# Grouped RMS norm of a two-layer hybrid decoder: one product with a matrix of 1/512 instead of two small steps, and the power of all 256 columns on GpSimd

## The chip, the cores and the metric

The kernel runs on one core of one Trainium2 chip. The time is that of one execution on the device in microseconds (us), from the first to the last instruction and what the runtime adds around it; less is better. The engines are named as in the profile: PE multiplies matrices (PEld loads its weights), DVE is VectorE, ACT is ScalarE, POOL is GpSimd, SP issues the loads.

## What is computed

Two layers, each on 256 tokens of width 1024. One input projection feeds an attention group (eight heads) and a state space group (SSD, sixteen heads); both results are gated, joined and multiplied by `w_out`. The change is in the norm that the SSD half passes before `w_out`. It works in two groups of 512 channels:

```python
y = y * jax.nn.silu(z.astype(jnp.float32))
y = rms_norm(y.reshape(b, s, SSD_GROUPS, D_SSD // SSD_GROUPS),
             ssd_norm_w.reshape(SSD_GROUPS, D_SSD // SSD_GROUPS))
...
mixed = jnp.concatenate([attn, y], axis=-1)
return x + mixed @ w_out
```

`rms_norm` multiplies by `lax.rsqrt(mean(x * x) + EPS)` and by a weight for each channel. For every token and group there is so one mean of 512 squares and one power of -0.5.

## The kernel before

Activations lie with channels on the 128 partitions and the 256 tokens along the free dimension. The SSD result is the tile `x2` (eight blocks of 128 channels by 256 tokens; the profile calls it `x`, as it calls the residual tile `x_sb`): group 0 is blocks 0 to 3, group 1 is blocks 4 to 7.

**Products in three parts.** A large product is made of three products each: activation and weight are split in a rounded part and a rest (`hT`/`lT`, `ah`/`al`, `sh`/`sl` for activations, `wh`/`wl` for weights), and high by high, low by high and high by low are added up in PSUM (lines 222 to 224, 240 to 242). ACT rounds each weight block from `raw` to `wh` (line 99), DVE subtracts to get `wl` (line 100). `Weights.pump` keeps at most eight blocks (`NB`) prepared that PE has not yet finished with; a block is two slices of 128 rows by up to 512 columns.

**Order of a layer's end.** The gates of attention are computed (`g`), then the gates of the SSD half (`z`, lines 653 to 659, four passes). After passes 1 and 3 the generator `group_norm` starts for group 0 and group 1. Then come the products with `w_out`: first all that need only the attention half (`oa0`, `oa1`: 96 products from `ah`, `al`), then `drain()` ends what generators are open, then 24 products `ob` (blocks 0 and 1 of `sh`, `sl`) and 72 products `oc` (blocks 2 to 7). In `oc` the first six products of a result take blocks 2 and 3, the rest blocks 4 to 7, which are group 1. The results lie in four tiles `o`; in the last layer one of them is cut in two of 256 columns, and the second half is called `o11b`.

**The norm itself.** `group_norm` (line 506) has three stages, divided by `yield 3` and `yield 2`, which put the next stage so many ticks later (a tick follows each weight block of PE). Stage one: ACT squares the four blocks (`ysq`), DVE adds the four (`sr`, 128 partitions by 256 tokens). Stage two: PE multiplies `sr` with a column of ones, which sums the 128 partitions and puts the tokens on the partitions (`np`, two products of one column each); DVE divides by 512 and adds epsilon (`nv`); POOL raises two columns to -0.5 (`rn`, helper `rpow`, line 181); DVE makes a diagonal matrix of it (`dg`). Stage three: PE multiplies `ones` by `dg`, which spreads the 256 powers to all partitions (`rg`, in PSUM); DVE multiplies each block of `x2` by the weight and by `rg` (line 533), and `split` (line 183) makes `sh` on ACT and `sl` on DVE for each two blocks.

`sr` and `dg` share one buffer (`tag="sr"`, one copy), so `sr` of group 1 waits until group 0 is done with it.

**What sets the order.** Every engine works through its own queue in order and waits by semaphores. The order in each queue is set when the program is built: a scheduler places each instruction by its own estimate of times, apart from the stretches under `manual_schedule` (the start, and PE's queue in the last `oc` products). A change in one place can therefore move instructions of other lines.

Of the kernel before, what the change touches and what calls it, by code (L numbers as in the profile page):

```python
# [9 lines left out]
F32 = mybir.dt.float32  # L10
F32R = mybir.dt.float32r
AF = mybir.ActivationFunctionType
ALU = mybir.AluOpType
AX = mybir.AxisListType

P = 128
S = 256
# [6 lines left out]
EPS = 1e-6  # L24
# [3 lines left out]
C_QN, C_KN, C_CW, C_CB, C_SW, C_DS, C_LN, C_DTB, C_AL = 0, 1, 2, 50, 62, 70, 78, 86, 102  # L28
# [91 lines left out]
def hybrid_kernel(ctx: ExitStack, tc: tile.TileContext, x, par, w, out):  # L120
    nc = tc.nc
    act, dve, pool, pe = nc.scalar, nc.vector, nc.gpsimd, nc.tensor

    const = ctx.enter_context(tc.tile_pool(name="const", bufs=1))
    keep = ctx.enter_context(tc.tile_pool(name="keep", bufs=1))
    tmp = ctx.enter_context(tc.tile_pool(name="tmp", bufs=2))
    small = ctx.enter_context(tc.tile_pool(name="small", bufs=4))
# [7 lines left out]
    def bank(name):  # L135
        return ps_s.tile([P, 512], F32, tag="ps_s", name=name)
# [4 lines left out]
    par_sb = const.tile([P, NL * NPAR], F32, name="par_sb")  # L141
# [12 lines left out]
    ones = const.tile([P, P], F32, name="ones")  # L154
# [5 lines left out]
    for i in range(WARM):  # L160
# [3 lines left out]
    io = tmp.tile([P, 512], F32, tag="th", name="io")  # L164
    pool.iota(io, pattern=[[1, 512]], base=-256, channel_multiplier=-1,
              allow_small_or_imprecise_dtypes=True)
    ident = const.tile([P, P], F32, name="ident")
    dve.tensor_scalar(ident, io[:, 256:384], 0.0, None, ALU.is_equal)
    tri = const.tile([P, 384], F32, name="tri")
# [6 lines left out]
    mhalf = const.tile([P, 8], F32, name="mhalf")  # L176
    dve.memset(mhalf, -0.5)

    def rpow(o, i):
        n = i.shape[-1]  # L180
        pool.tensor_tensor(o, i, mhalf[:, :n], ALU.pow)

    def split(h, l, src):
        act.copy(h, src)
        dve.tensor_tensor(l, src, h.bitcast(F32), ALU.subtract)
# [320 lines left out]
    def group_norm(L, g, y, sh, sl):  # L506
        pc = L * NPAR
        gs = slice(4 * g, 4 * g + 4)
        sq = tmp.tile([P, 4, S], F32, tag="sq", name="ysq", bufs=1)
        act.activation(sq, y[:, gs, :], AF.Square)  # L510
        sr = tmp.tile([P, S], F32, tag="sr", name="sr", bufs=1)
        dve.tensor_reduce(sr, sq.rearrange("p c n -> p n c"), AX.X, ALU.add)
        yield 3
        np_ = bank("np")
        for t in range(2):
            pe.matmul(np_[:, t:t + 1], sr[:, t * P:(t + 1) * P], ones[:, 0:1],
                      start=True, stop=True)
        nv = small.tile([P, 2], F32, tag="nv", name="nv")
        dve.tensor_scalar(nv, np_[:, 0:2], 1.0 / 512.0, 4.0 * EPS, ALU.mult, ALU.add)
        rn = small.tile([P, 2], F32, tag="rn", name="rn")  # L520
        rpow(rn, nv)
        dg = tmp.tile([P, S], F32, tag="sr", name="dg", bufs=1)
        for t in range(2):
            ts = slice(t * P, (t + 1) * P)
            dve.tensor_scalar(dg[:, ts], ident, rn[:, t:t + 1], None, ALU.mult)
        yield 2
        rg = bank("rg")
        for t in range(2):
            ts = slice(t * P, (t + 1) * P)
            pe.matmul(rg[:, ts], ones, dg[:, ts], start=True, stop=True)  # L530
        for c in range(4):
            ct = 4 * g + c
            dve.scalar_tensor_tensor(y[:, ct, :], y[:, ct, :],
                                     par_sb[:, pc + C_SW + ct:pc + C_SW + ct + 1], rg[:, 0:256],
                                     ALU.mult, ALU.mult)
            if c % 2:
                split(sh[:, ct - 1:ct + 1, :], sl[:, ct - 1:ct + 1, :], y[:, ct - 1:ct + 1, :])
# [3 lines left out]
    for L in range(NL):  # L541
        pc = L * NPAR
# [110 lines left out]
        for pr in range(4):  # L653
            ps = ps_p.tile([P, 512], F32, tag="ps_p", name=f"z{pr}")
            mm_pair(L, f"z{pr // 2}", pr % 2, hT, lT, ps, pr % 2 == 1)
            ys = x2[:, 2 * pr:2 * pr + 2, :]
            dve.tensor_tensor(ys, ys, silu2(ps), ALU.mult)
            if pr % 2 == 1:
                resume(group_norm(L, pr // 2, x2, sh, sl))
# [101 lines left out]
```

## Time and profile before

| | us |
|---|---|
| median of three runs (455.07 to 455.64) | 455.21 |
| the profiled execution | 456.82 |
| span of its instructions | 455.0 |
| PE busy in the span | 445.7 (98%) |
| DVE busy | 345.9 (76%) |
| ACT busy | 278.5 (61%) |
| POOL busy | 23.7 (5%) |

The profile is one execution. Its busy time counts instructions that do work, not semaphores; the end of a PE product is modelled, so products that follow each other overlap in the rows, and the distance from start to start tells the rate. A row of the timeline gives the start, the duration, the engine, the line and what is written from what; in square brackets stands the idle time before it and what ended it. DVE and POOL rows give the time of the instruction itself.

### The profile page before, as it was taken

The page shows a single profiled execution, that of the slowest core. Times are in us where ns is not written, and L with a number is a line of the kernel's source. Part 1 is how long each engine was busy: PE and PEld are TensorE (multiplying, and loading weights), DVE is VectorE, ACT ScalarE, POOL GpSimd, SP SyncE. Part 2 cuts the span into 40 slices and gives each one's busy share as a digit, 9 for nine tenths or more (in the row PEclk, how much of TensorE's full clock was granted, in tenths as well). Part 3 has the DMA queues.
Part 4 walks back from the last instruction along what each step waited for, and adds up shares of the span by engine and source line. Part 5 has one row for each costly group of instructions (what it writes and reads, how often), then busy time and mean ns, then how long its engine had stood idle before and what let it go on. Part 6 is the DMA issues. An engine that isn't in the chain of part 4 may idle for free.

```text
span 455.0 us, 7868 instructions
## 1 busy us (share of the span) xinstructions
PE 445.7 (98%) x2948; PEld 404.1 (89%) x2948; DVE 345.9 (76%) x634; ACT 278.5 (61%) x569; POOL 23.7 (5%) x29
## 2 busy tenths in 40 slices
PE   7999999999999999999999999999999999999997
PEld 6998877899998999888899878889999999998986
DVE  5597873789999998778384785676999999787621
ACT  5666775996669545445365766967667765555400
POOL 0000221200000000000000011110000000000000
PEclk9999999999999999999999999999999999999999
DMA  8868767524453445555264888651525443553301
GB/s 248 289 226 289 257 234 303 177 89 149 145 180 119 130 150 185 186 176 146 57 184 159 297 288 306 205 184 52 178 90 171 157 140 117 183 185 128 130 24 69
DMA packets 26661, 79.43 MB, mean 175 GB/s; under 512 B 2912, under 2 KB 9728, under 8 KB 26112
## 3 DMA queue, kind: packets, MB, share of 16 engines
q1 hardware_dynamic: 26192, 78.67, 52.2%
q8 instruction: 23, 0.38, 0.3%
q10 hardware_dynamic: 432, 0.27, 0.2%
q14 instruction: 14, 0.11, 0.1%
HBM read 77.85 MB, written 1.08 MB: 173 GB/s over the span
## 4 chain that ended last, share of the span: by engine, by line
PE 86%; DMA 5%; ACT 4%; DVE 3%; issue 2%; POOL 1%; ACTq 0%; SPq 0%; DVEq 0%; POOLq 0%
PE o L222 6%; PE o L223 6%; PE o L224 6%; PE xb L240 4%; PE xb L242 4%; PE xb L241 4%; PE z L241 3%; PE z L240 3%; PE z L242 3%; PE g L242 3%; PE g L240 3%; PE g L241 3%; PE yp L491 3%; PE k L222 2%; PE q L222 2%; PE k L223 2%
## 5 line engine op out<-in xcount | busy, mean ns | idle before, releaser
L100 DVE TENSOR_TENSOR wl<-raw,wh 128x1024 fp32r<-128x1024 f32 (+3 forms) x145 | 165.5, 1156 | 40.3 <-ACT wh L99 38.6
L99 ACT CAST wh<-raw 128x1024 fp32r<-128x1024 f32 (+3 forms) x145 | 143.3, 999 | 60.0 <-DMA raw<-in_w_dram 19.2
L240 PE MATMUL xb<-hT,wh 128*128 128x256 f32 x192 | 56.1, 292 | 0.0
L241 PE MATMUL xb<-lT,wh 128*128 128x256 f32 x192 | 54.4, 284 | 0.0
L242 PE MATMUL xb<-hT,wl 128*128 128x256 f32 x192 | 53.6, 279 | 0.0
L241 PEld LDWEIGHTS xb<-lT,wh 128*128 128x128 f32 x192 | 36.2, 189 | 0.3
L240 PEld LDWEIGHTS xb<-hT,wh 128*128 128x128 f32 x192 | 36.1, 188 | 0.2
L242 PEld LDWEIGHTS xb<-hT,wl 128*128 128x128 f32 x192 | 36.1, 188 | 0.1
L242 PE MATMUL g<-hT,wl 128*128 128x256 f32 x128 | 36.1, 282 | 0.0
L241 PE MATMUL z<-lT,wh 128*128 128x256 f32 x128 | 36.1, 282 | 0.0
L240 PE MATMUL g<-hT,wh 128*128 128x256 f32 x128 | 36.0, 281 | 0.0
L240 PE MATMUL z<-hT,wh 128*128 128x256 f32 x128 | 36.0, 281 | 0.0
L242 PE MATMUL z<-hT,wl 128*128 128x256 f32 x128 | 36.0, 281 | 0.0
L241 PE MATMUL g<-lT,wh 128*128 128x256 f32 x128 | 35.9, 281 | 0.0
L440 DVE SCALAR_TENSOR_TENSOR cv<-rw,par_sb,cv 128x256 f32<-128x256 f32 x72 | 31.6, 478 | 5.1 <-ACT cv L437 5.1
L222 PE MATMUL k<-wh,hT 128*128 128x512 f32 x64 | 25.5, 399 | 0.0
L223 PE MATMUL k<-wh,lT 128*128 128x512 f32 x64 | 25.3, 396 | 0.0
L224 PE MATMUL k<-wl,hT 128*128 128x512 f32 x64 | 25.3, 395 | 0.0
L222 PE MATMUL q<-wh,hT 128*128 128x512 f32 x64 | 25.3, 397 | 0.0
L223 PE MATMUL q<-wh,lT 128*128 128x512 f32 x64 | 25.0, 393 | 0.0
L224 PE MATMUL q<-wl,hT 128*128 128x512 f32 x64 | 24.7, 396 | 0.0
L222 PE MATMUL o<-wh,ah 128*128 128x512 f32 (+1 forms) x64 | 24.6, 384 | 0.0
(194 smaller groups left out, 1104.4 us busy)
## 6 DMA issues: line engine op xcount, KB each, us to landing
raw<-in_w_dram SPq DMA_DIRECT2D x120, 512.0 KB, 4.3
raw<-in_w_dram SPq DMA_DIRECT2D x15, 348.0 KB, 3.8
cb<-cd SPq DMA_DIRECT2D x4, 1024.0 KB, 7.2
raw<-in_w_dram SPq DMA_DIRECT2D x8, 344.0 KB, 3.8
x<-in_x_dram SPq DMA_DIRECT2D x2, 512.0 KB, 6.2
xT<-in_w_dram SPq DMA_DIRECT2D x3, 256.0 KB, 4.9
out_dram<-x SPq DMA_DIRECT2D x3, 256.0 KB, 2.0
raw<-in_w_dram SPq DMA_DIRECT2D x2, 174.0 KB, 3.4
```

The lines of the kernel that those rows point to most:

```text
L99: nc.scalar.copy(h[:, ks, :wd], src[:, ks, :wd])
L100: nc.vector.tensor_tensor(lo[:, ks, :wd], src[:, ks, :wd], h[:, ks, :wd].bitcast(F32), ALU.subtract)
L222: pe.matmul(ps[:, cs], lh[:, kl, tl], wh[:, kk, cs], start=first, stop=False)
L223: pe.matmul(ps[:, cs], ll[:, kl, tl], wh[:, kk, cs], start=False, stop=False)
L224: pe.matmul(ps[:, cs], lh[:, kl, tl], wl[:, kk, cs], start=False, stop=final)
L240: pe.matmul(o, wh[:, kk, cs], lh[:, k, :], start=(k == 0 and c == 0), stop=False)
L241: pe.matmul(o, wh[:, kk, cs], ll[:, k, :], start=False, stop=False)
L242: pe.matmul(o, wl[:, kk, cs], lh[:, k, :], start=False, stop=(k == KT - 1 and c == 1))
L440: dve.scalar_tensor_tensor(cv[:, c, :], rw[:, c, k:k + S], cw(k), cv[:, c, :], ALU.mult, ALU.add)
L491: pe.matmul(yp[o, c0:(i + 1) * S], xd[:, hi, xs], e_hi[:, j, :] if hi else e_lo[:, j, :], start=(hi == 0), stop=(hi == 1))
```

## The change

The sum over partitions and its spreading become one product: a 128 by 128 matrix filled with 1/512 (`ones512`) times `sr` puts the mean of each token on all partitions at once (`np`, 256 columns). DVE adds epsilon and writes the result to SBUF as `rg`, in the buffer of `sr`. POOL raises `rg` to -0.5 in place, 128 partitions by 256 columns, the exponent read from one column of `mhalf`. DVE then multiplies from this `rg`, which lies in SBUF and no longer in PSUM. The steps `nv`, `rn`, `dg` and the product `rg` are gone. `ones512` is filled once at the start.

```diff
+    ones512 = const.tile([P, P], F32, name="ones512")
+    dve.memset(ones512, 1.0 / 512.0)
...
         np_ = bank("np")
-        for t in range(2):
-            pe.matmul(np_[:, t:t + 1], sr[:, t * P:(t + 1) * P], ones[:, 0:1],
-                      start=True, stop=True)
-        nv = small.tile([P, 2], F32, tag="nv", name="nv")
-        dve.tensor_scalar(nv, np_[:, 0:2], 1.0 / 512.0, 4.0 * EPS, ALU.mult, ALU.add)
-        rn = small.tile([P, 2], F32, tag="rn", name="rn")
-        rpow(rn, nv)
-        dg = tmp.tile([P, S], F32, tag="sr", name="dg", bufs=1)
-        for t in range(2):
-            ts = slice(t * P, (t + 1) * P)
-            dve.tensor_scalar(dg[:, ts], ident, rn[:, t:t + 1], None, ALU.mult)
+        pe.matmul(np_[:, 0:S], ones512, sr, start=True, stop=True)
+        rg = tmp.tile([P, S], F32, tag="sr", name="rg", bufs=1)
+        dve.tensor_scalar(rg, np_[:, 0:S], 4.0 * EPS, None, ALU.add)
+        pool.tensor_tensor(rg, rg, mhalf[:, 0:1].to_broadcast([P, S]), ALU.pow)
         yield 2
-        rg = bank("rg")
-        for t in range(2):
-            ts = slice(t * P, (t + 1) * P)
-            pe.matmul(rg[:, ts], ones, dg[:, ts], start=True, stop=True)
         for c in range(4):
...
-                                     par_sb[:, pc + C_SW + ct:pc + C_SW + ct + 1], rg[:, 0:256],
+                                     par_sb[:, pc + C_SW + ct:pc + C_SW + ct + 1], rg,
```

The change also moves instructions of other lines, because the scheduler places them anew. Line numbers of the changed program are two higher from the helper `rpow` on and nine lower behind `group_norm`; the numbers behind the names are those of buffers.

DVE's queue in layer 1 before, from the epsilon step `nv` of group 0 on (`wl` is the weight rest, `g2z` and the `x` behind it the gate of pass 3, line 533 the norm's multiplications):

```order
L519 TENSOR_SCALAR nv<-np 128x2
L100 TENSOR_TENSOR wl_4775<-raw_4643,wh_4774 128x1024
L525 TENSOR_SCALAR dg<-ident,rn 128x128 x2
L100 TENSOR_TENSOR wl_4803<-raw_4736,wh_4802 128x1024
L503 SCALAR_TENSOR_TENSOR g2z<-thz,z_4712 128x512
L657 TENSOR_TENSOR x_1_3433<-x_1_3433,g2z 128x512
L533 SCALAR_TENSOR_TENSOR x_1_3433<-x_1_3433,par_sb,rg 128x256 x4
L512 TENSOR_REDUCE sr<-ysq 128x256
```

The same stretch of DVE's queue in the changed program:

```order
L519 TENSOR_SCALAR rg<-np 128x256
L100 TENSOR_TENSOR wl_4753<-raw_4629,wh_4752 128x1024
L100 TENSOR_TENSOR wl_4781<-raw_4714,wh_4780 128x1024
L505 SCALAR_TENSOR_TENSOR g2z<-thz,z_4693 128x512
L648 TENSOR_TENSOR x_1_3419<-x_1_3419,g2z 128x512
L100 TENSOR_TENSOR wl_4831<-raw_4732,wh_4830 128x1024
L100 TENSOR_TENSOR wl_4843<-raw_4750,wh_4842 128x1024
L100 TENSOR_TENSOR wl_4855<-raw_4778,wh_4854 128x1024
L100 TENSOR_TENSOR wl_4868<-raw_4828,wh_4867 128x1024
L524 SCALAR_TENSOR_TENSOR x_1_3419<-x_1_3419,par_sb,rg 128x256 x4
L187 TENSOR_TENSOR sl_4491<-x_1_3419,sh_4490 128x512
L514 TENSOR_REDUCE sr<-ysq 128x256
```

Four more subtractions `wl` now stand between the epsilon step and the norm's multiplications; in layer 0 it is eight more. Behind the epsilon step of group 1 stand one `wl` (layer 0, of 696 columns) and three (layer 1) ahead of the multiplications.

PE's queue in layer 0 before, around the partition sums `np` of group 1 (`ah`, `al` are the attention half):

```order
L223 MATMUL o_2421<-wh_2283,al_1718 128x512
L224 MATMUL o_2421<-wl_2284,ah_1717 128x512
L516 MATMUL np<-ones,sr 128x1 x2
L222 MATMUL o_2421<-wh_2283,ah_1717 128x512
L223 MATMUL o_2421<-wh_2283,al_1718 128x512
```

And in the changed program (`sh`, `sl` are the normed SSD half; `wh_2385` belongs to `ob`, `wh_2397` is the first block of `oc`):

```order
L225 MATMUL o_2438<-wh_2385,sl_2034 128x512
L226 MATMUL o_2438<-wl_2386,sh_2033 128x512
L224 MATMUL o_2438<-wh_2385,sh_2033 128x512
L517 MATMUL np<-sr,ones_120 128x256
L225 MATMUL o_2438<-wh_2385,sl_2034 128x512
L226 MATMUL o_2438<-wl_2386,sh_2033 128x512
L224 MATMUL o_2320<-wh_2397,sh_2033 128x512
L225 MATMUL o_2320<-wh_2397,sl_2034 128x512
```

The product `np` of group 1 stood among the products of the attention half; it now stands behind 22 products that read the normed group 0. In layer 1 it is 23 of them, and the 24 products of `o11b` from `ah` and `al` stand behind it.

## Rows read from the trace of the kernel before

**Rows 1.** The page, part 1: busy us, share and count by engine.
```profile
PE 445.7 (98%) x2948; PEld 404.1 (89%) x2948; DVE 345.9 (76%) x634; ACT 278.5 (61%) x569; POOL 23.7 (5%) x29
```

**Rows 2.** POOL's groups by shape: count | busy us, mean ns | idle before, releaser.
```profile
L181 POOL TENSOR_TENSOR rr<-se,mhalf 128x4 f32<-128x4 f32 x16 | 18.0, 1124 | 123.0 <-DVE se L337 89.7 <-DVE dt L401 33.3
L181 POOL TENSOR_TENSOR rn<-nv,mhalf 128x2 f32<-128x2 f32 x4 | 2.8, 697 | 223.7 <-DVE nv L519 223.7
L181 POOL TENSOR_TENSOR rs<-me,mhalf 128x1 f32<-128x1 f32 x4 | 2.2, 560 | 51.5 <-DVE me L256 32.1 <-DVE me L302 19.4
L165 POOL IOTA io<- 128x512 f32 x1 | 0.6, 557 | 0.4 <-POOLq L746 0.4
```

**Rows 3.** POOL's timeline: start us, us, instruction, idle before.
```profile
50.80 2.02 POOL L181 TENSOR_TENSOR rr<-se,mhalf 128x4 f32<-128x4 f32 x1 [1.56 <-DVE se L337]
...
184.54 0.69 POOL L181 TENSOR_TENSOR rn<-nv,mhalf 128x2 f32<-128x2 f32 x1 [94.52 <-DVE nv L519]
201.04 0.69 POOL L181 TENSOR_TENSOR rn<-nv,mhalf 128x2 f32<-128x2 f32 x1 [15.80 <-DVE nv L519]
...
270.51 1.01 POOL L181 TENSOR_TENSOR rr<-se,mhalf 128x4 f32<-128x4 f32 x1 [1.27 <-DVE se L337]
```

**Rows 4.** DVE's timeline at the norm of layer 0, group 0.
```profile
184.31 0.15 DVE L519 TENSOR_SCALAR nv<-np 128x2 f32<-128x2 f32 x1
184.59 1.23 DVE L100 TENSOR_TENSOR wl<-raw,wh 128x1024 fp32r<-128x1024 f32 x1
...
186.45 1.23 DVE L100 TENSOR_TENSOR wl<-raw,wh 128x1024 fp32r<-128x1024 f32 x1 [0.24 <-ACT wh L99]
...
188.31 0.69 DVE L657 TENSOR_TENSOR x<-x,g2z 128x512 f32<-128x512 f32 x1
191.52 1.66 DVE L533 SCALAR_TENSOR_TENSOR x<-x,par_sb,rg 128x256 f32<-128x256 f32 x4 [2.52 <-PE rg L530]
...
197.41 3.48 DVE L100 TENSOR_TENSOR wl<-raw,wh 128x1024 fp32r<-128x1024 f32 x3
```

**Rows 5.** DVE's timeline elsewhere: beside two powers of Rows 3, and layer 1.
```profile
50.73 1.22 DVE L100 TENSOR_TENSOR wl<-raw,wh 128x1024 fp32r<-128x1024 f32 x1
...
270.56 1.23 DVE L100 TENSOR_TENSOR wl<-raw,wh 128x1024 fp32r<-128x1024 f32 x1 [0.19 <-ACT wh L99]
...
404.97 0.15 DVE L519 TENSOR_SCALAR nv<-np 128x2 f32<-128x2 f32 x1
405.69 1.22 DVE L100 TENSOR_TENSOR wl<-raw,wh 128x1024 fp32r<-128x1024 f32 x1 [0.57 <-ACT wh L99]
```

**Rows 6.** ACT's timeline at the norm of layer 0.
```profile
189.09 1.06 ACT L510 ACTIVATE ysq<-x 128x1024 f32<-128x1024 f32 x1 [2.19 <-DVE x L657]
192.43 0.62 ACT L184 CAST sh<-x 128x512 fp32r<-128x512 f32 x1 [2.27 <-DVE x L533]
```

**Rows 7.** PE's timeline: first `ob` product and first of group 1, both layers.
```profile
208.76 0.39 PE L222 MATMUL o<-wh,sh 128*128 128x512 f32 x1
...
215.62 0.39 PE L222 MATMUL o<-wh,sh 128*128 128x512 f32 x1
...
426.71 0.28 PE L222 MATMUL o11b<-wh,ah 128*128 128x256 f32 x1
...
429.54 0.40 PE L222 MATMUL o<-wh,sh 128*128 128x512 f32 x1
...
436.47 0.39 PE L222 MATMUL o<-wh,sh 128*128 128x512 f32 x1
```

**Rows 8.** The chain in order of time: start us, us, what.
```profile
191.04 0.44 PE rg L530 x4
```

**Rows 9.** DVE's groups by shape: an operation of 256 columns that reads PSUM.
```profile
L692 DVE TENSOR_TENSOR x<-x,o 128x256 f32<-128x256 f32 x1 | 0.4, 422 | 1.4 <-PE o L224 1.4
```

**Rows 10.** The page, part 2 (granted clock, tenths), and PE's first timeline row.
```profile
PEclk9999999999999999999999999999999999999999
...
1.05 4.64 PE L161 MATMUL warm<-ones 128*128 128x128 f32 x20 [1.05 <-DVE ones L155]
```

## The prediction

> **What bounds the kernel now.** I read the page first: PE is busy for 445.7 of 455.0 us, POOL for 23.7 [rows 1]. So a change counts only where it makes PE wait or takes work from PE. Then the timelines around the two norms of each layer. In layer 0 the power `rn` of group 0 ends at 185.2 [rows 3], the norm's multiplications run from 191.52 [rows 4], and PE takes the normed blocks only at 208.76 [rows 7]: some 15 us of slack. Group 1 has its power at 201.04 [rows 3], and PE takes its first block at 215.62 [rows 7]. Nothing of the norm makes PE wait today. What the change adds must fit in that slack, or it is paid in full.
>
> **What POOL will charge.** The same operation takes 560 ns for one column, 697 for two [rows 2], and 1.01 us for four when undisturbed [rows 3] (the mean of 1124 [rows 2] holds disturbed ones as well). That is 137 ns for the second column and some 155 for each of the next two: the price of a column does not fall with length in these rows. To 256 columns: 560 + 255 x 149 (the mean step) = 38.6 us; by the last step, 1007 + 252 x 155 = 40.1 us; by the smallest, 697 + 254 x 137 = 35.5 us. I take 39.4, between the first two, as four columns are the nearest row. It stands four times, so one microsecond here is four at the end.
>
> **Group 0, layer 0.** The epsilon step starts where `nv` did, at 184.31 [rows 4]. It now writes 256 columns from PSUM: 0.42 us by the nearest such row [rows 9] in place of 0.15, so it ends at 184.73. POOL followed `nv` by 0.08 us [rows 3, 4], so the power starts at 184.81 and ends at 224.2. The first cast `sh` starts 0.91 us after the first multiplication [rows 4, 6] and takes 0.62; with 0.14 for the hand-overs from POOL to DVE and from ACT to PE (a guess, of the size of that 0.08) it is 1.67 us, so the first product with `sh` is at 225.9 and not at 208.76. PE's other work ends at about 207.7 there, as the products `rg`, 0.44 us each [rows 8], are gone. PE waits 18 us.
>
> **Group 1, layer 0.** This no longer runs beside. Its sum `sr` lies in the buffer that holds `rg` until group 0's multiplications have read it, and stands behind them on DVE; on PE its `np` stands behind 22 products that need group 0. Thirty such products took from 208.76 to 215.62 [rows 7], 0.229 each, so 22 take 5.0 and `np` runs at 230.9. A product of 256 columns is as long as the four passes of 128 of `rg`, 0.44 [rows 8]; with its pipeline I let DVE start 0.6 later. Then 0.42 + 0.08, and the power starts at 232.1 and ends at 271.5; with the 1.67 the first product of group 1 is at 273.1, which was at 215.62. PE has only eight products (1.8 us) to do meanwhile. **Layer 0 costs 57.5 us.**
>
> **Layer 1**, in its own old times: 404.97 [rows 5] + 0.42 + 0.08 + 39.4 gives 444.9, first `sh` product 446.5 (it was 429.54). Then 18 products of 512 columns and 5 of 256 (0.118 each: 24 from 426.71 to 429.54 [rows 7]), 4.7 us; then 0.6 + 0.5 + 39.4 + 1.67, which is 493.4 against 436.47 [rows 7]. **Layer 1 costs 57.0 us.** The 24 products `o11b`, now behind `np`, are done in this wait and cost nothing; on the path they would be 2.8 us.
>
> **Clock.** The page shows the full granted clock all through [rows 10]. Yet the first 20 passes of 128 columns took 4.64 us after a PE that had done nothing [rows 10], against 0.11 us each in mid-kernel [rows 8], which makes 2.2: at the start PE went at half its speed for 4 us and lost about 2. Here PE starts four times after a wait of 18 to 39 us. Lower bound 0 (the trace has no such wait), upper bound twice the row's loss, 16 in all; I take 2 each, 8 us.
>
> **What goes away** is worth almost nothing: 0.44 us of `rg` on PE and two `dg` on DVE for each group lie ahead of waits that PE now has anyway. The `memset` of `ones512` stands ahead of `mhalf` while DVE waits for POOL's first output; hidden.
>
> Sum so far, against the profiled execution's own time: 456.8 + 57.5 + 57.0 + 8 = 579.3. The median lies 1.6 below that execution, so 577.7.
>
> **What DVE does meanwhile decides the rest.** In layer 0 ten `wl` subtractions and the gate's product stand behind the epsilon step and ahead of the multiplications; all read two operands from SBUF. The row at 50.80 is a power that started 0.07 us after such a subtraction: 2.02 us instead of 1.01 [rows 3, 5]. It waited until the subtraction had read its operands. The other way round, a subtraction that started 0.05 us after a power kept its 1.23 us, though the power ran on for 0.96 [rows 3, 5], and so did the one at 184.59 [rows 4]. But these powers may have read their two or four columns at once; one of 256 columns reads for as long as it computes, unless it first copies its input. So either the two exclude each other for 39 us, or hardly at all; the trace has no power of this length. I hold exclusion the more likely, since one direction of it is seen.
>
> If they exclude each other: in layer 0 the first `wl` stands ready (it ran at 184.59 [rows 4]) and starts just before the power, which waits 1.0 us and ends at 225.2. PE meanwhile runs out of `wl` blocks near 200, but it would have waited anyway. From 225.2 DVE does one `wl`, `g2z` and `x`, 2.5 us as from 186.45 to 189.0 [rows 4], ACT squares (1.06 [rows 6]) and casts as many elements (about as long), and eight `wl` follow at 1.13 us (three took 3.48 [rows 4]), ending at 239.0. Only then come the multiplications: 14.8 us later than 224.2. Group 1 of layer 0 has one short `wl`: 0.7. In layer 1 the power wins (its `wl` waits for ACT until 405.69 [rows 5]); two `wl`, gate, square, cast, then four `wl`: 455.2 against 444.9, 10.3. Group 1 there has three `wl`: 3.4. Sum 29.2, so 608.5 by the profile, **606.9** by the median. If DVE slips in and only stops POOL for as long as it reads, the same subtractions lengthen the powers by about 24: 602.
>
> The Trainium skill, "SBUF — State Buffer", "Who interferes with whom", says that a DVE instruction with two SBUF inputs contends with a GpSimd instruction that reads SBUF, and that whoever holds the shared pair first blocks the other for the whole instruction. The row at 50.80 agrees; the row at 270.56 does not, for a power of four columns; of 256 columns no run here shows it. By the rule the time would be 606.9, without it 577.7.
>
> **Rivals.** *No exclusion*: 577.7 us, everything as above, with DVE's work hidden under the power. The row at 270.56 speaks for it [rows 5], the one at 50.80 against it [rows 3]. *A loop that is cheaper for long rows*: at a quarter of the price, 10 us, group 0 is hidden (184.8 + 10 + 1.7 is before 207.7), and group 1 waits 10.6 us in layer 0 (10 + 2.4 less 1.8 of cover) and 7.4 in layer 1 (5 of cover); with some 2 us of clock loss and 1.3 of PE work gone, 474. Against it: the steps of 137, 155, 155 ns. *Not slower*: POOL's one long instruction in the trace, 512 columns, takes 557 ns [rows 2]. If the 560 ns of a one-column power are fixed cost and the steps an effect of tiny operands, the power takes about 0.7 us; then only group 1 of layer 0 waits, 0.7 + 2.4 - 1.8 = 1.3 us, PE saves 1.3 us, and the time is 455.2. It decides below about 2 us. Against it: that instruction computes no power and reads nothing.
>
> The Trainium skill, "GPSIMD Engine Reference", "3.1 Elementwise — side-by-side cycle accounting", gives 4497 ns for an addition of 2048 columns; by that an operation of 256 columns would be an estimated 0.6 us and the change free. The rows contradict it for this operation, with 137 to 155 ns for a column [rows 2].
>
> **How the numbers follow.** Exclusion 0.57 (0.45 with DVE blocked, 0.12 with POOL stopped), no exclusion 0.29, cheaper loop 0.09, not slower 0.05. The forecast is 606.9. Its own range: 3 us either way for the power's price, 8 for the clock, so 596 to 618. Eight in ten must reach to the case without exclusion, 577.7 less 11, so the range is 567 to 618. Slower by over 0.2% (0.9 us, about what a measurement of this kernel can tell from no change): 0.95; same 0.04; faster 0.01.
>
> **What would show it.** The row of POOL's line 520: near 39 us is the main step; 0.7 or 10 us are the rivals. Four PE waits: before the first `sh` product of each layer, and before group 1's. Whether `wl` rows inside a power last 1.2 us or tens of us, or whether the power itself grows, tells exclusion. The rate of the products after each wait tells the clock. Wrong altogether: `np` of group 1 starting before group 0's power has ended.

## The result: 587.3 us against 455.4

| us | before | changed |
|---|---|---|
| median (four runs each) | 455.39 | 587.28 |
| lowest and highest | 455.07, 455.64 | 586.55, 588.31 |
| profiled execution | 456.82 | 586.68 |
| span | 455.0 | 584.9 |

The changed kernel takes 1.290 times as long (95% interval 1.288 to 1.292). The time lies inside the predicted range of 567 to 618 and 19.6 us below the forecast of 606.9. The rival without exclusion (577.7) named the mechanism; its powers and its clock loss were set somewhat too cheap. That the range holds the time is not to the credit of the main forecast, whose mechanism did not occur: the range had been stretched downwards to reach that rival.

The page of the changed kernel: busy us, share and count by engine; then granted clock and POOL's busy share in 40 slices of the span; then the chain that ended last, by engine; then POOL's new group.

```profile
PE 455.1 (78%) x2924; PEld 410.3 (70%) x2924; DVE 346.9 (59%) x627; ACT 280.3 (48%) x569; POOL 187.3 (32%) x29
...
POOL 0002120000005993998000111100000089939940
PEclk8999999999999955655899999999999998575559
...
PE 67%; POOL 21%; POOLq 7%; DVE 2%; ACT 1%; DMA 1%; issue 0%; ACTq 0%; DVEq 0%
...
L520 POOL TENSOR_TENSOR rg<-rg,mhalf 128x256 f32<-128x256 f32 x4 | 165.4, 41351 | 213.5 <-DVE rg L519 213.5
```

Against [rows 1], DVE and ACT are about as busy as before. POOL has 163.6 us more, which are the four powers (165.4) less the small ones that are gone (2.8 [rows 2]), and 0.9 more for the small powers `rr` (18.9 against 18.0 [rows 2]). PE has 9.4 us more of busy time with 24 instructions fewer: the granted clock, full all through before [rows 10], falls to 5 tenths in two stretches. Each of these lies where POOL's row shows two blocks of 9, that is, at the end of a layer.

POOL's timeline in the changed kernel (start us, us, instruction, idle before and what ended it), where [rows 3] had powers of 0.69 us:

```profile
182.45 42.04 POOL L520 TENSOR_TENSOR rg<-rg,mhalf 128x256 f32<-128x256 f32 x1 [95.23 <-DVE rg L519]
234.86 41.12 POOL L520 TENSOR_TENSOR rg<-rg,mhalf 128x256 f32<-128x256 f32 x1 [10.37 <-DVE rg L519]
...
469.52 41.13 POOL L520 TENSOR_TENSOR rg<-rg,mhalf 128x256 f32<-128x256 f32 x1 [97.65 <-DVE rg L519]
520.93 41.12 POOL L520 TENSOR_TENSOR rg<-rg,mhalf 128x256 f32<-128x256 f32 x1 [10.28 <-DVE rg L519]
```

PE's waits in the changed kernel (who waits for whom: us in total, times, longest), the first of the list:

```profile
PE o L224 <- ACT sh L186: 123.3, 4, 41.5
```

This is 123.3 of the 131.9 us between the medians; the rest is work that PE does at a lower rate. Each engine is released by the one before it: POOL's power releases DVE's multiplication, DVE releases ACT's cast, ACT releases PE's product. PE's wait names ACT, but ACT itself has waited all that time, so the cost belongs at the head of the line. The four waits are 20.6, 41.5, 22.8 and 38.3 us.

The chain in order of time, from group 0's epsilon step of layer 0 to the first products after group 1 (start us, us, what):

```profile
181.96 0.43 DVE rg L519
182.45 42.05 POOL rg L520
224.53 0.89 DVE x L524 x2
225.44 0.63 ACT sh L186
226.11 2.08 PE o L224 x4
...
233.82 0.45 PE np L517 x2
234.29 0.44 DVE rg L519
234.86 41.13 POOL rg L520
276.01 0.89 DVE x L524 x2
276.92 0.63 ACT sh L186
277.59 0.79 PE o L224
```

The chain's shares on the page fit this: 21% of 584.9 us are three powers, and the 7% of `POOLq` are the length of the fourth. No subtraction `wl` stands in the chain between the power and the multiplications; the prediction had put eight of them there. DVE's timeline shows where they are: inside the power.

```profile
182.29 1.21 DVE L100 TENSOR_TENSOR wl<-raw,wh 128x1024 fp32r<-128x1024 f32 x1
...
206.40 1.23 DVE L100 TENSOR_TENSOR wl<-raw,wh 128x1024 fp32r<-128x1024 f32 x1 [0.17 <-ACT wh L99]
224.53 1.67 DVE L524 SCALAR_TENSOR_TENSOR x<-x,par_sb,rg 128x256 f32<-128x256 f32 x4 [16.90 <-POOL rg L520]
```

The row at 182.29 began before the power; those after it keep their 1.23 us while POOL works up to 224.49, and DVE is idle for 16.9 us before the multiplications.

After each wait PE is slow. PE's timeline behind group 1's wait, with the first products and those where the distance changes:

```profile
277.59 0.79 PE L224 MATMUL o<-wh,sh 128*128 128x512 f32 x1 [41.50 <-ACT sh L186]
...
281.49 0.63 PE L226 MATMUL o<-wl,sh 128*128 128x512 f32 x1
281.92 0.63 PE L224 MATMUL o<-wh,sh 128*128 128x512 f32 x1
...
283.11 0.39 PE L225 MATMUL o<-wh,sl 128*128 128x512 f32 x1
283.33 0.39 PE L226 MATMUL o<-wl,sh 128*128 128x512 f32 x1
```

And a table of the same stretches (window, then busy us and count for PE, PEld, DVE, ACT, POOL, then the granted clock, the share of the DMA engines and GB/s):

```profile
210.00:225.00 15.00, 0.00 (x0) 0.00 (x0) 0.47 (x2) 0.00 (x0) 14.49 (x1) 0.50 0.04 15
...
280.00:285.00 5.00, 5.00 (x18) 3.96 (x18) 0.69 (x1) 0.72 (x2) 0.00 (x0) 0.75 0.00 0
285.00:290.00 5.00, 5.00 (x24) 4.09 (x23) 1.51 (x3) 1.88 (x4) 0.56 (x1) 1.00 0.00 0
```

While PE waits the granted clock is at 0.50, that is 1.2 of 2.4 GHz. When products come again the first gaps are 0.75 and 0.59 us (0.6 us of the two together is not the clock's: where PE was kept busy they are 0.74 and 0.34), then they stand 0.43 us apart up to about 282.4, and 0.23 from there on. The first eleven gaps take 5.06 us, where eleven of 0.229 would take 2.5.

### The profile page after: what moved, and what is told of

Same layout as the page of the kernel before. It is cut to its first block, busy times and chain, and to the rows that moved or that the text cites. A ratio compares the mean times of both kernels' runs of the same rounds, so it can differ in the third digit from the quotient of the medians.

```text
span 584.9 us, 7812 instructions
## 1 busy us (share of the span) xinstructions
PE 455.1 (78%) x2924; PEld 410.3 (70%) x2924; DVE 346.9 (59%) x627; ACT 280.3 (48%) x569; POOL 187.3 (32%) x29
## 4 chain that ended last, share of the span: by engine, by line
PE 67%; POOL 21%; POOLq 7%; DVE 2%; ACT 1%; DMA 1%; issue 0%; ACTq 0%; DVEq 0%
POOL rg L520 21%; POOLq L747 7%; PE xb L242 4%; PE xb L244 4%; PE xb L243 4%; PE o L224 3%; PE v L224 3%; PE v L225 3%; PE v L226 3%; PE o L225 3%; PE k L224 3%; PE k L225 3%; PE q L226 3%; PE g L244 3%; PE g L242 3%; PE q L225 3%
## 5 line engine op out<-in xcount | busy, mean ns | idle before, releaser
L520 POOL TENSOR_TENSOR rg<-rg,mhalf 128x256 f32<-128x256 f32 x4 | 165.4, 41351 | 213.5 <-DVE rg L519 213.5
L224 PE MATMUL o<-wh,sh 128*128 128x512 f32 (+1 forms) x64 | 28.2, 460 | 123.3 <-ACT sh L186 123.3
L224 PEld LDWEIGHTS o<-wh,sh 128*128 128x128 f32 x64 | 14.6, 232 | 127.6 <-ACT sh L186 124.8
L524 DVE SCALAR_TENSOR_TENSOR x<-x,par_sb,rg 128x256 f32<-128x256 f32 x16 | 6.7, 478 | 120.6 <-POOL rg L520 120.6
L186 ACT CAST sh<-x 128x512 fp32r<-128x512 f32 x8 | 4.9, 618 | 130.0 <-DVE x L524 130.0
L183 POOL TENSOR_TENSOR rr<-se,mhalf 128x4 f32<-128x4 f32 x16 | 18.9, 1182 | 119.1 <-DVE se L339 119.1
L225 PE MATMUL o<-wh,sl 128*128 128x512 f32 (+1 forms) x64 | 28.0, 438 | 0.0
```

The costliest lines, as they stand in the source:

```text
L224: pe.matmul(ps[:, cs], lh[:, kl, tl], wh[:, kk, cs], start=first, stop=False)
L225: pe.matmul(ps[:, cs], ll[:, kl, tl], wh[:, kk, cs], start=False, stop=False)
L520: pool.tensor_tensor(rg, rg, mhalf[:, 0:1].to_broadcast([P, S]), ALU.pow)
```

## The experiments

The theory after the result: four powers of 41.1 us stand in full on the path, priced by their columns; DVE and POOL do not hinder each other; each restart of PE costs 2.4 us. The rivals: the price is by elements or partitions; the powers are slowed by DVE; group 1's place in the queues costs time apart from its power; the change has some other cost of its own (one product with the matrix of 1/512, the multiplications from SBUF).

### Half the columns

```diff
-        pool.tensor_tensor(rg, rg, mhalf[:, 0:1].to_broadcast([P, S]), ALU.pow)
+        pool.tensor_tensor(rg[:, 0:128], rg[:, 0:128], mhalf[:, 0:1].to_broadcast([P, 128]), ALU.pow)
```

> The changed kernel with the power taken on the first 128 of the 256 columns only; the other 128 columns are left without it. Theory (the power costs 159 ns for every further column and PE waits for it): from 1.0 us for four columns and 41.1 for 256, 128 columns take 20.8 us. In layer 0 the power of group 0 is then nearly hidden (PE waits 2 to 3 us), that of group 1 leaves a cost of 24 us; layer 1 costs 20 us; with two restarts of PE at half clock (2.4 us each) the time is about 504 us. Rival (a fixed cost of a long power, or DVE's work shut out for as long as a power runs): the power stays well above 21 us and the time well above 520.

Measured: 507.98 us (one run). POOL's timeline of this kernel:

```profile
183.25 21.64 POOL L520 TENSOR_TENSOR rg<-rg,mhalf 128x128 f32<-128x128 f32 x1 [96.38 <-DVE rg L519]
220.12 20.72 POOL L520 TENSOR_TENSOR rg<-rg,mhalf 128x128 f32<-128x128 f32 x1 [15.23 <-DVE rg L519]
```

The price follows the columns: 20.4 us less for 128 fewer, 159 ns for each. Its four waits are 45.1 us in all, 78.2 less than with 256 columns, against 79.3 by which the time is shorter. The time is 4 us above what was expected: PE's busy time is 452.6 us, 8.4 above that of the kernel with sixteen columns (444.2), where the expectation had 4.8 for two restarts. One of the reasons is seen at the first wait of layer 0, which lasts only 2.3 us:

```profile
208.52 1.19 PE L224 MATMUL o<-wh,sh 128*128 128x512 f32 x4 [2.26 <-ACT sh L186]
210.40 0.80 PE L225 MATMUL o<-wh,sl 128*128 128x512 f32 x1 [0.69 <-DVE sl L187]
211.00 0.63 PE L226 MATMUL o<-wl,sh 128*128 128x512 f32 x1
211.42 0.63 PE L224 MATMUL o<-wh,sh 128*128 128x512 f32 x1
```

Four products still go at the full rate, a second wait of 0.69 us follows, and then they stand 0.43 us apart, as after the long waits. In this run, waits of 2.26 and 0.69 us were enough for the loss at half rate.

### Sixteen columns

The same edit with 16 in place of 128.

> The changed kernel with the power taken on the first 16 of the 256 columns only; the rest is left without it. Theory: the power takes 2.9 us and lies under the attention half's products, so that only what else the change does is left: about 0.7 us less PE work a layer, 453.9 us against 455.3 before. Rival (the new product, the epsilon step from PSUM, or the multiplications that now read two operands from SBUF cost something themselves): 456 us or more.

Measured: 451.90 us (450.69 to 452.40) against 454.63 for the kernel before on the same chip, ratio 0.993 (0.991 to 0.996). The powers take 2.89 and 2.90 us, in layer 0 3.81 and 3.74. PE never waits for this norm. With the power short, nothing else of the change costs anything: the product with 1/512, the multiplications from SBUF and the new order are free or better. This rules out the last rival. It came out 2 us faster than expected. PE's busy time is 444.2 us against 445.7 [rows 1], which accounts for 1.5 of the 2.7 us below the kernel before; the rest is not accounted for.

This run is also the frame against which the changed kernel's time closes. Its span is 450.6 us; the changed kernel has 123.3 us of waits and 10.9 us more of PE's busy time (455.1 against 444.2, for the same 2924 instructions, so all of it lower rate): 450.6 + 123.3 + 10.9 = 584.8, and its span is 584.9. Within the scatter of the runs that leaves nothing for any other cause: all that PE waits for besides is as long in both, 6.4 and 6.5 us.

### The same norm without POOL

ACT takes the root of the mean plus epsilon straight from PSUM, DVE the reciprocal. This computes the full result.

```diff
-        dve.tensor_scalar(rg, np_[:, 0:S], 4.0 * EPS, None, ALU.add)
-        pool.tensor_tensor(rg, rg, mhalf[:, 0:1].to_broadcast([P, S]), ALU.pow)
+        act.activation(rg, np_[:, 0:S], AF.Sqrt, bias=epsb)
+        dve.reciprocal(rg, rg)
```

> The changed kernel with one product of 1/512, but without GpSimd: ACT takes the square root straight from PSUM with epsilon as bias, DVE the reciprocal of 256 columns. Theory (the loss is POOL's price alone): both steps lie in the slack of 15 us that the norm had before, and the time is that of the 16-column kernel, about 453.9 us, 0.3% below the kernel before. Rival (ACT has to change its function tables for the square root and back, and its casts of the weights come late): up to 1.5 us for each of eight changes, 12 us, if they fall where PE waits for casts.

Measured: 453.68 us (12 runs, 452.69 to 455.78) against 454.63 for the kernel before (17 runs), ratio 0.998 (0.9965 to 0.9994). So the first half of the change, one product that sums and spreads, is worth a little at best, when the power is taken elsewhere. Its groups (count | busy us, mean ns | idle before):

```profile
L521 ACT ACTIVATE rg<-np,epsb 128x256 f32<-128x256 f32 x4 | 1.9, 474 | 4.6 <-PE np L519 4.6
L522 DVE RECIPROCAL rg<-rg 128x256 f32<-128x256 f32 x4 | 7.0, 1753 | 4.5 <-ACT rg L521 4.5
...
L521 ACT ACT_TABLE_LOAD x4 | 5.1, 1283 | 0.1
```

The same 128 by 256 powers take 0.47 + 1.75 us here, or 3.5 with the table load of 1.28 us that each root brings, against 41.1 on POOL. After the roots other functions load tables again (three such loads, where the kernel before has one at the start and no other), all on an engine that is 64% busy. The gain over the kernel before is 1 us, at the edge of what can be told.

### Both powers one behind the other

`rg` gets one of the two `cm` buffers, so that group 1's sum `sr` need not wait for group 0.

```diff
-        rg = tmp.tile([P, S], F32, tag="sr", name="rg", bufs=1)
+        rg = tmp.tile([P, 384], F32, tag="cm", name="rg")[:, 0:S]
```

> The changed kernel with a buffer of its own (two copies) for the result of the epsilon step, so that the sum of group 1 need not wait for group 0; the program's order then has the partition sums of group 1 among the products of the attention half again. Theory (POOL itself is the bound, 41 us for each of two powers a layer): the second power follows the first at once, 10.3 us earlier than now in each layer, and the time is 587.3 - 20.6 = 567 us. Rival (the shared buffer is the cause, and two powers could hide if they started early): below 520 us.

Measured: 567.41 us (one run). POOL's timeline shows both powers of a layer as one row, without a gap:

```profile
183.69 83.12 POOL L520 TENSOR_TENSOR rg<-rg,mhalf 128x256 f32<-128x256 f32 x2 [96.46 <-DVE rg L519]
```

In layer 1 it is one row of 82.21 us. The shared buffer therefore costs 20 us: the 10.4 and 10.3 us in which POOL stood idle between the two powers of a layer. That is the part of the price which is neither the power itself nor PE's lower rate, and the prediction had it ("no longer runs beside").

### PE kept busy during group 1's wait

```diff
+        for _ in range((181, 167)[L]):
+            pe.matmul(dw[:, 0:P], ones, ones, start=True, stop=True)
```

These products stand before those that need group 1; nothing reads `dw`.

> The changed kernel with idle products of 128 columns (ones by ones, read by nobody) on PE during the wait for group 1's power: 181 in layer 0 and 167 in layer 1, at 0.222 us each 40 and 37 us, a little less than the wait. Theory (after each wait PE goes at half its clock for some 5 us and loses 2.4 us): both restarts after group 1's power are at full clock, 587.3 - 4.8 = 582.5 us. Rival (the clock costs nothing on the path): 587 us, or more if the idle products overrun the wait.

Measured: 582.06 us (581.47 to 582.59), ratio 1.279 (1.276 to 1.283), 5.2 below the changed kernel, for two of the four waits. PE's timeline: from the third product on they stand 0.23 apart, and the mean granted clock of the execution is 0.961 against 0.883.

```profile
278.03 0.50 PE L224 MATMUL o<-wh,sh 128*128 128x512 f32 x1 [1.07 <-ACT sh L186]
...
279.11 0.40 PE L226 MATMUL o<-wl,sh 128*128 128x512 f32 x1
279.35 0.39 PE L224 MATMUL o<-wh,sh 128*128 128x512 f32 x1
```

Here the second product comes 0.74 us after the first, since it waits for `sl`, so the start is slow even at the full clock. Against the changed kernel the first eleven gaps in layer 0 take 3.16 us and not 5.06, the first twelve in layer 1 3.38 and not 5.58. The two restarts that the idle products replaced therefore cost 1.9 and 2.2 us, 4.1 together, where 4.8 had been expected and the prediction's 2 for each makes 4. They are not all of the 5.2: the profiled executions differ by 4.2 us, and 0.9 of that comes from elsewhere, for the wait ahead of group 0 in layer 1, 22.81 us in both, was followed by a shorter stretch at half rate.

### A ladder of powers in a place where nobody waits

In the kernel before, layer 0, behind a `cm` step, on a tile that nothing else reads: 8, 16, 32, 64 and 128 columns on 128 partitions, then 64 columns on 16 partitions.

```diff
+                        for n in (8, 16, 32, 64, 128):
+                            pool.tensor_tensor(lad[:, 0:n], lad[:, 0:n],
+                                               mhalf[:, 0:1].to_broadcast([P, n]), ALU.pow)
+                        pool.tensor_tensor(lad[0:16, 0:64], lad[0:16, 0:64],
+                                           mhalf[0:16, 0:1].to_broadcast([16, 64]), ALU.pow)
```

> The kernel before with six more powers on POOL in its idle stretch of layer 0, on a tile that nobody reads: 8, 16, 32, 64 and 128 columns of 128 partitions, then 64 columns of 16 partitions. Theory (159 ns for each further column, a row of up to 128 partitions at a time): 1.6, 2.9, 5.5, 10.6, 20.8 us, and for 16 partitions the same 10.6 us as for 128. Rival (the price falls with length, or is paid for each element): 128 columns well under 20 us, or 64 columns of 16 partitions near an eighth of 10.6. The time stays within 1 us of before, 455 us, if DVE's work beside these powers is not held up; where DVE and POOL shut each other out, DVE's rows there grow and the time rises.

Measured: 454.88 us (one run) against 455.23 before; the work is hidden. POOL's groups by shape:

```profile
L638 POOL TENSOR_TENSOR lad<-lad,mhalf 128x128 f32<-128x128 f32 x1 | 20.8, 20798 | 0.1
...
L640 POOL TENSOR_TENSOR lad<-lad,mhalf 16x64 f32<-16x64 f32 x1 | 11.2, 11192 | 0.1
L638 POOL TENSOR_TENSOR lad<-lad,mhalf 128x64 f32<-128x64 f32 x1 | 10.5, 10524 | 0.1
...
L638 POOL TENSOR_TENSOR lad<-lad,mhalf 128x16 f32<-128x16 f32 x1 | 3.7, 3697 | 0.1
L638 POOL TENSOR_TENSOR lad<-lad,mhalf 128x8 f32<-128x8 f32 x1 | 2.9, 2945 | 20.7 <-DVE lad L636 20.7
```

Sixteen partitions cost as much as 128. By elements, 16 by 64 would be the price of eight columns on all partitions. So the price is by column, whatever the number of partitions. The 64 and the 128 columns came out as expected; 8, 16 and 32 columns and the one of 16 partitions 0.6 to 1.3 us above. At each of those four starts DVE's timeline has an instruction with two operands in SBUF under way; here at 8 columns (start at 108.74) and at 16 columns (start at 111.8):

```profile
108.58 0.48 DVE L440 SCALAR_TENSOR_TENSOR cv<-rw,par_sb,cv 128x256 f32<-128x256 f32 x1
108.97 1.22 DVE L100 TENSOR_TENSOR wl<-raw,wh 128x1024 fp32r<-128x1024 f32 x1
...
111.50 1.21 DVE L100 TENSOR_TENSOR wl<-raw,wh 128x1024 fp32r<-128x1024 f32 x1
```

The power of 16 columns needs 2.9 us by the experiment with 16 columns. It started 0.9 before that subtraction's end and took 0.8 more. That of 16 by 64 (start at 153.27) started 0.83 before the end of a subtraction that ran from 152.87, and took 0.67 more than 128 by 64. The power of 8 columns took 1.3 more than the 1.64 that 159 ns a column give. The instruction under way at its start ends at 109.06, which is too soon for that; the subtraction that DVE began behind it, 0.23 us after the power's own start, ends at 110.19, and 0.14 before that end fits. So here a waiting power was passed by DVE's next instruction as well.

### Many two-operand additions on DVE inside a power

Sixty additions that read two operands from SBUF, behind the epsilon step of group 1, layer 0, on a tile that nothing else reads.

```diff
+        if L == 0 and g == 1:
+            dm = tmp.tile([P, 384], F32, tag="cm", name="dm")
+            dve.tensor_copy(dm[:, 0:S], np_[:, 0:S])
+            for _ in range(60):
+                dve.tensor_tensor(dm[:, 0:S], dm[:, 0:S], base[:, 0:S], ALU.add)
```

> The changed kernel with 60 additions of 256 columns on DVE, both operands in SBUF (some 25 us), queued behind the epsilon step of group 1 in layer 0 and ahead of the norm's multiplications, that is inside a power of 41 us, on a tile that nobody reads. Theory (a power under way and a DVE instruction with two SBUF operands don't disturb each other): the power stays at 41.1 us, the additions at 0.4 us each, and the time at 587 us. Rival (they shut each other out): the power grows by up to 25 us, or the additions run only after it; 612 us either way.

Measured: 587.07 us (one run), the time of the changed kernel. POOL's and DVE's timelines:

```profile
235.81 41.12 POOL L520 TENSOR_TENSOR rg<-rg,mhalf 128x256 f32<-128x256 f32 x1 [9.49 <-DVE rg L519]
...
236.03 0.67 DVE L525 TENSOR_TENSOR dm<-dm,base 128x256 f32<-128x256 f32 x1
...
237.43 26.99 DVE L525 TENSOR_TENSOR dm<-dm,base 128x256 f32<-128x256 f32 x59
```

All but the first of the additions ran at 0.46 us from one to the next (26.99 over 59), from 237.4 to 264.4, and the power over them took 41.12 us, to the hundredth what it took without them. By itself such an addition lasts 0.42 us in the middle of the 60 values; the one on `base` at the start of the program (line 177), where no power runs, lasts 0.42 too. Only the first, which began 0.22 us after the power, took 0.67, a quarter of a microsecond more. From then on neither engine held the other up. This settles the step that the forecast and its rival differed on.

## Why the prediction was right, and where it failed

**Right: that nothing of the norm made PE wait, and that the slack was some 15 to 18 us.** Group 0's wait in layer 0 was put at 18 us. It was 20.6. The power was 2.64 longer than the 39.4 assumed (42.04), and that is the whole difference.

**Right: group 1 behind group 0.** From the first product with `sh` to that of group 1 the prediction had 47.2 us (225.9 to 273.1); it was 51.5 (226.11 to 277.59). Of the 4.3 more, 1.7 are the power and 2.5 the half rate of the products ahead of `np`, which the sum had under clock; 0.1 is left. Layer 1: 46.9 predicted, 51.4 measured, by the same two terms. The experiment with own buffers shows the order's part alone, 20 us over both layers.

**The step that failed: "I hold exclusion the more likely, since one direction of it is seen".** This added 29.2 us to the forecast; on the path it is worth the 0.9 us by which the first power of layer 0 stood back behind a subtraction (the exclusion case had 1.0 for that) and nothing else. Of the two rows that the prediction weighed, the one at 50.80 shows what happens when the power comes second, the one at 270.56 what happens when DVE comes second [rows 3, 5]. Both were right as they stood, and they do not contradict each other: the changed kernel repeats each of them. Only the extension from the first to a whole power of 39 us was wrong. The price of the wrong case was worked out properly. Its chance, 0.57 against 0.29, rested on the row at 50.80, whose order is not that of the case in question (DVE's instruction arriving while POOL works). The row at 270.56 has that order, but with four columns it could not tell the two cases apart, as the prediction says itself: a long power either reads as long as it computes, "unless it first copies its input". The rows at the start of the long powers now speak for the second. A `wl` that began 0.19 us after a power of 256 columns and one that began 0.20 us after a power of 128 (start at 434.72):

```profile
469.71 1.50 DVE L100 TENSOR_TENSOR wl<-raw,wh 128x1024 fp32r<-128x1024 f32 x1 [0.28 <-ACT wh L99]
...
434.92 1.28 DVE L100 TENSOR_TENSOR wl<-raw,wh 128x1024 fp32r<-128x1024 f32 x1 [0.28 <-ACT wh L99]
```

Elsewhere a `wl` takes 1.21 to 1.23, and with a power of 16 columns it took 1.23 at the same distance. So DVE was held back until some 0.47 us into the power of 256 columns and 0.26 into that of 128, and not after. Exclusion was there, but for half a microsecond in place of 39. That POOL reads its columns in that time is the likely reading, not one that these runs show.

The Trainium skill, "SBUF — State Buffer", "Who interferes with whom", says that the engine which comes first blocks the other for its whole instruction. The rows agree for a power that comes second. For a DVE instruction that comes second they agree for the first half microsecond alone: the additions and `wl` rows that began later ran through powers of 41 us at their usual time, and the measurement decides.

**Mis-sized: the price of the power.** 39.4 us was taken, between 38.6 by the mean step and 40.1 by the last step; it measured 41.12. The step from four columns on is 159 ns ((41.12 - 1.01) / 252, the 1.01 from [rows 3]). The steps in the trace went 137, 155, 155: they still grew, and the last one was the better guide. The upper bound of 40.1 was itself 1 us too low. Four times 1.7 are 6.9 us, and the first power of layer 0 took another 0.9.

**Mis-sized: the clock.** From the first product after each wait to where they stand 0.23 us apart again, the rows lose 2.5, 2.5, 2.6 and 2.8 us against 0.229 for each 512 columns. That is 10.5 against the 8 of the sum, 2.5 more, of which the wait of the second product for `sl` behind group 1 makes some 1.2; what is the clock's is 1.9 to 2.6 for each restart.

The rival without exclusion with these three corrections is 577.7 + 6.9 + 0.9 + 2.5 = 588.0 against the measured 587.28, a median of runs from 586.55 to 588.31. The terms at zero were right, as the run with sixteen columns shows: the product with 1/512, the epsilon step of 256 columns, the multiplications from SBUF.

The Trainium skill, "GPSIMD Engine Reference", "3.1 Elementwise — side-by-side cycle accounting", was weighed as a price for an elementwise instruction: by an addition's cost the power would be an estimated 0.6 us. It was right to set the rows of the same operation above it, since that gave 39.4 for 41.1.

**Where the frame was off.** The prediction took its times from the profiled execution before, whose epsilon step of layer 0 was at 184.31 [rows 4]; in the changed kernel it is at 181.96. Two waits of PE account for it. The profiled execution before lists PE's waits as (us in total, times, longest):

```profile
PE pp L373 <- DVE sc L368: 1.5, 1, 1.5
...
PE sp L355 <- ACT kT L348: 0.8, 1, 0.8
```

Neither is in the changed kernel, nor in the run of the kernel before with the ladder, whose program is nearly the same (the scheduler moved some instructions there too). So they are most likely of that execution and not of its order of instructions, and then taking 1.6 us off for the median was right.

## What to carry to other kernels

Before values are spread so that "one instruction does it all", ask what the instruction charges for: here 159 ns for a column whatever the number of partitions, so 256 tokens cost two columns when they lie on the partitions and 256 when they lie along the free dimension with 128 copies of each. When two rows seem to speak for opposite rules, look at which operation came first in each, let the row decide whose order is that of the case at hand, and ask whether that row is long enough to tell. And price a wait on PE together with its restart: each of these cost 1.9 to 2.6 us beyond its length.

## What was not expected of the hardware

A power on POOL that starts while DVE runs an instruction with two operands in SBUF works only from some 0.14 us before that instruction's end, and in one case before that of the next (the power of 8 columns). In the changed kernel the subtraction at 182.29 ends at 183.50, and the power at 182.45 took 0.92 more than the others. With sixteen columns, subtractions started at 182.63 and 195.89 with 1.22 us, and powers at 182.79 and 196.12 took 0.92 and 0.85 more than the 2.89 of layer 1. A DVE instruction with two operands in SBUF that starts inside a power is held only in its beginning: 0.25 to 0.28 us where it began 0.2 us after a power of 256 columns, 0.35 where a multiplication of the run with own buffers began 0.06 after one (0.83 us at 225.76, where 0.48 is usual), 0.06 for 128 columns. Later ones pay nothing. Why is not shown by these runs.

A power of 16 partitions was as long as one of 128. After a wait in which PE did nothing, products went at half rate for 4.8 to 5.6 us in the changed kernel, after 20 us as after 41 us (granted clock 0.50); in another run, after waits of 2.26 and 0.69 us, they fell to it too; and they kept the full rate where PE had been given products to do in the wait.

The run with sixteen columns was 1.2 us faster than PE's shorter busy time accounts for; where that comes from is open.
